# Eight columns of the conditioning product moved from VectorE to TensorE, x in four transfers, a shorter Newton step

## The chip, the cores and the metric

The kernel runs on one core of a Trainium2 chip. The time is the device time of one execution in microseconds, the median of several runs. In the views, PE is TensorE's matmuls, PEld its weight loads, DVE is VectorE, ACT ScalarE, POOL GpSimd, and SP the engine whose queue issues the transfers.

## What is computed

One layer of a streaming encoder on x of 512 tokens by 1024 features: a token-mixing half and a half with retrieved experts, each behind a normalization that is conditioned by a vector c. What the change touches is the conditioning and the norms:

```python
ada = c @ w_ada[layer] + b_ada[layer]
shift1, scale1, gate1, shift2, scale2, gate2 = [a[:, None, :] for a in jnp.split(ada, 6, axis=-1)]
h = rms_norm(x, g_norm1[layer]) * (1.0 + scale1) + shift1
z = h @ w_in[layer]
```

with `rms_norm(x, g) = x * rsqrt(mean(x * x) + EPS) * g`. ada has 6 x 1024 elements; the kernel holds it as 48 columns of 128.

## The kernel before

Features lie on the partitions, tokens along the free axis. x comes transposed as eight blocks `xs[:, d, :]` of 128 features by 512 tokens. `layer` is recorded as a program whose order on each engine a scheduler sets, within the dependencies; stretches that must keep their order are pinned.

The first stage (lines 241 to 285) makes the modulated input in two parts, `hh` and `hl`, a value rounded for the fast f32 format and what the rounding left, and multiplies it with five blocks of `w_in`, split in the same way into `whs` and `wls`. Each block and each feature block k gives three passes (`passes`, L171 to L173), 5 x 8 x 3 = 120 passes over 512 columns, into five banks `ps0` to `ps4`.

For feature block d the stage needs two columns of ada, the scale in column 8 + d and the shift in column d. `ada_col` (L102) loads 128 rows of the transposed w_ada as a tile `wada`, [128, 1024], and DVE multiplies it with c and sums along the row (L106). For that c is needed on all partitions: it comes as one row, `crow`, PE multiplies it with a column of ones (L253), and ACT copies the two halves into `cb` (L254). DVE then adds the bias (L266), makes a1 = (1 + scale) * g (L267) and, in `modulate`, x * a1 * r (L156); ACT adds the shift and rounds, giving `hh` (L157), and DVE makes `hl` (L158). The tiles `wada` rotate over four buffers, so a transfer waits for the product that read the buffer four columns before.

r, the reciprocal root, comes from `rsqrt` (L125): PE sums the squares over the partitions with a matrix of ones into `n1s` (L150, L151), ACT takes a logarithm, an exponential and a square, and DVE does one Newton step in three instructions (L132 to L134). It is used for the first norm (n1), for the norms of the index keys (nik), keys (nk) and queries (nq), and for the second norm (n2).

SP issues the transfers of this stage in order: `col` (constants by feature), `crow`, the eight blocks of x, then for each d two columns of w_ada and one block of w_in (`ws`), while there are any. The remaining 32 columns of ada come later, spread over the attention stages as background work.

After this stage come the queries, keys, scores and attention, the output projection, the second norm (from L500, where x is loaded again as `x2T`), and the experts, which take the larger part of the time.

## Time and profile before

| | us |
|---|---|
| median of 3 runs (1542.19 to 1545.64) | 1543.28 |
| the profiled execution | 1543.97 |
| its span, first to last instruction | 1542.2 |
| PE busy in it | 1496.3 (97%) |
| DVE busy | 1293.7 (84%) |
| ACT busy | 646.2 (42%) |

Busy time of PE is an upper bound, since matmuls are pipelined and their ends are modelled. The chain of waits that ended last runs over PE for 81% of the span, over DVE for 11%. All times of the rows below are microseconds from the start of the span, unless marked ns. A reader who looks at one stage should ask of each engine what it waited for there, and what its next instruction in order is.

### The profile page before, as it was taken

To read this page: it belongs to the slowest core of one execution; us is meant where nothing else is said; L and a number is where in the kernel's file an instruction comes from. 1 tells how busy PE (TensorE), PEld (TensorE's weight loads), DVE (VectorE), ACT (ScalarE), POOL (GpSimd) and SP (SyncE) were. 2 spreads that over 40 slices of the span, in tenths; PEclk is the share of its full clock that TensorE was granted. 3 is DMA by queue.
4 is the path that set the end of the run, shared out by engine and by line. 5 is a ranking of instruction groups with operands and counts; after the bars stand their busy time and mean duration, and the time that the engine had idled before them with its cause. 6 is when DMAs were issued, how large, how long until landed. Compare 5 with 4: busy or idle time off the path is not lost.

```text
span 1542.2 us, 22240 instructions
## 1 busy us (share of the span) xinstructions
PE 1496.3 (97%) x7889; PEld 1301.6 (84%) x7889; DVE 1293.7 (84%) x2672; ACT 646.2 (42%) x991; POOL 324.4 (21%) x318
## 2 busy tenths in 40 slices
PE   5999999999899999999999999999999999999998
PEld 3678788877799989899888999999999999998886
DVE  7799786667999999993778888888888888888887
ACT  4643555443345554463333333333333333333332
POOL 0000000000000000001123444444444444453320
PEclk8999999999999999999999999999999999999999
DMA  8422663532236656789889999999999999998884
GB/s 313 164 82 77 216 227 105 191 117 96 71 122 205 195 176 208 221 254 318 325 317 354 333 343 360 317 362 318 356 348 330 359 318 363 333 349 315 312 305 144
DMA packets 158545, 393.91 MB, mean 255 GB/s; under 512 B 13537, under 2 KB 68449, under 8 KB 158306
## 3 DMA queue, kind: packets, MB, share of 16 engines
q1 hardware_dynamic: 121570, 258.26, 48.3%
q0 software_dynamic: 36864, 134.23, 24.6%
q8 instruction: 62, 1.02, 0.3%
q14 instruction: 49, 0.40, 0.1%
HBM read 358.75 MB, written 33.69 MB: 254 GB/s over the span
## 4 chain that ended last, share of the span: by engine, by line
PE 81%; DVE 11%; DMA 5%; ACT 2%; issue 1%; SPq 0%; ACTq 0%; DVEq 0%
PE acc L806 28%; PE pse L555 6%; PE pse L554 6%; PE pse L553 6%; PE pse L569 4%; PE pse L571 4%; PE pse L570 3%; PE gm L666 3%; DMA v<-v 3%; DVE ule L533 2%; PE po L470 1%; DVE vl L798 1%; PE pso L171 1%; PE psgp L173 1%; PE psgp L171 1%
## 5 line engine op out<-in xcount | busy, mean ns | idle before, releaser
L731 POOL DMA_INDIRECT ur<-u,ei x128 | 156.3, 1221 | 603.5 <-DMA ad<-gelu 365.4
L806 PE MATMUL acc<-vl,Wh 128*128 128x512 f32 x768 | 237.1, 390 | 0.7 <-DVE vl L798 0.7
L806 PE MATMUL acc<-vh,Wl 128*128 128x512 f32 x768 | 237.3, 390 | 0.0
L806 PE MATMUL acc<-vh,Wh 128*128 128x512 f32 x768 | 236.8, 389 | 0.0
L739 POOL DMA_INDIRECT vr<-v,ei x128 | 165.2, 1290 | 213.7 <-DVE sacc L744 185.1
L798 DVE TENSOR_TENSOR vl<-v,vh 128x1024 fp32r<-128x1024 f32 x128 | 156.8, 1225 | 63.2 <-ACT vh L796 52.0
L555 PE MATMUL pse<-h2h,ule 128*128 128x384 f32 x552 | 185.2, 336 | 0.7 <-DVE ule L533 0.7
L553 PE MATMUL pse<-h2h,uhe 128*128 128x384 f32 x552 | 184.5, 334 | 0.6 <-ACT uhe L532 0.6
L554 PE MATMUL pse<-h2l,uhe 128*128 128x384 f32 x552 | 184.7, 335 | 0.0
L795 ACT ACTIVATE Wh<-gelu 128x384 fp32r<-128x384 f32 x106 | 55.6, 525 | 286.2 <-PE acc L806 161.9
L806 PEld LDWEIGHTS acc<-vl,Wh 128*128 128x128 f32 x768 | 143.9, 188 | 31.7 <-DVE vl L798 2.0
L806 PEld LDWEIGHTS acc<-vh,Wl 128*128 128x128 f32 x768 | 144.2, 188 | 29.9
L569 PE MATMUL pse<-h2h,uhe 128*128 128x384 f32 x472 | 167.8, 355 | 0.6 <-ACT gelu L578 0.6
L533 DVE TENSOR_TENSOR ule<-ue,uhe 128x1024 fp32r<-128x1024 f32 x128 | 155.8, 1217 | 13.7 <-ACT uhe L532 13.5
L571 PE MATMUL pse<-h2h,ule 128*128 128x384 f32 x472 | 161.1, 342 | 4.8 <-DVE ule L533 4.8
L744 DVE SCALAR_TENSOR_TENSOR sacc<-vr,wt,sacc 128x1024 f32<-128x1024 f32 x127 | 162.8, 1282 | 2.4
L806 PEld LDWEIGHTS acc<-vh,Wh 128*128 128x128 f32 x768 | 143.2, 188 | 24.7 <-ACT vh L796 0.3
L570 PE MATMUL pse<-h2l,uhe 128*128 128x384 f32 x472 | 159.1, 337 | 0.0
L532 ACT ACTIVATE uhe<-ue 128x1024 fp32r<-128x1024 f32 x128 | 134.5, 1051 | 57.8 <-PE pse L570 42.3
L733 DVE SCALAR_TENSOR_TENSOR ur<-ur,hx 128x1024 f32<-128x1024 f32 x128 | 150.6, 1218 | 0.4 <-DMA ur<-u,ei 0.4
L796 ACT ACTIVATE vh<-v 128x1024 fp32r<-128x1024 f32 x128 | 135.8, 1061 | 15.5 <-DMA v<-v 15.4
L553 PEld LDWEIGHTS pse<-h2h,uhe 128*128 128x128 f32 x552 | 103.6, 188 | 3.6 <-ACT uhe L532 1.0
(422 smaller groups left out, 2669.3 us busy)
## 6 DMA issues: line engine op xcount, KB each, us to landing
ue<-uT SPq DMA_DIRECT2D x128, 512.0 KB
v<-v SPq DMA_DIRECT2D x128, 512.0 KB
wada<-w_ada SPq DMA_DIRECT2D x48, 512.0 KB
gd<-st SPq DMA_DIRECT2D x24, 1024.0 KB
g<-gd SPq DMA_DIRECT2D x48, 512.0 KB
ad<-gelu SPq DMA_DIRECT2D x22, 192.0 KB
wgp<-w_in SPq DMA_DIRECT2D x8, 512.0 KB
wga<-w_in SPq DMA_DIRECT2D x8, 512.0 KB
```

The lines of the kernel that those rows point to most:

```text
L533: V.tensor_tensor(lo, src, hi.bitcast(F32), op=ALU.subtract)
L553: T.matmul(p, hi[:, k, :], h2h[:, k, :n], start=(k == 0), stop=False)
L554: T.matmul(p, hi[:, k, :], h2l[:, k, :n], start=False, stop=False)
L555: T.matmul(p, lo[:, k, :], h2h[:, k, :n], start=False, stop=(k == DT - 1))
L569: T.matmul(ps, hi[:, k, :], h2h[:, k, :ND], start=(k == 0), stop=False)
L570: T.matmul(ps, hi[:, k, :], h2l[:, k, :ND], start=False, stop=False)
L571: T.matmul(ps, lo[:, k, :], h2h[:, k, :ND], start=False, stop=(k == DT - 1))
L731: G.indirect_dma_start(out=ur, out_offset=None, in_=u, in_offset=bass.IndirectOffsetOnAxis(ap=ei3[:, k:k + 1], axis=0))
L739: G.indirect_dma_start(out=vr, out_offset=None, in_=v, in_offset=bass.IndirectOffsetOnAxis(ap=ei3[:, k:k + 1], axis=0))
L744: V.scalar_tensor_tensor(sacc, vr, wt[:, k:k + 1], sacc, op0=ALU.mult, op1=ALU.add)
L798: V.tensor_tensor(vl, vr, vh.bitcast(F32), op=ALU.subtract)
L806: T.matmul(acc[tb][i], x[:, t], y[:, i * 512:(i + 1) * 512], start=(c == 0 and n == 0), stop=(c == NEXP - 1 and n == 2))
```

## The change

Four edits:

- The columns of ada for the feature blocks 0 to 3 (`NPE = 4`) are made on PE. The host arranges their parts of w_ada so that a tile `wadp` holds, for each of the eight blocks k of c, 128 rows by 128 columns; PE takes each as the weights and one column of c, which now comes with `col`, as the moving operand (`ada_product`, L265 after the change), 8 matmuls into one column of the bank `pad`. DVE adds the bias from there. Blocks 4 to 7 stay with DVE as they were. The row `crow` and its two products follow only at d = 3, in one bank.
- x comes in four transfers of two blocks each, here and before the second norm, from an array arranged for it.
- The Newton step takes two instructions. Its factor -0.5 * scale is multiplied into the gains beforehand (L104, L105 of the changed kernel) and into the factor of rq.
- `col` is eight columns wider.

```diff
--- before.py
+++ after.py
@@ -59,7 +59,9 @@
 
 
 C_G1, C_G2, C_GQ, C_GK, C_GIK, C_SP, C_BADA = 0, 8, 16, 17, 18, 19, 23
-NCOLS = C_BADA + 48
+C_C = C_BADA + 48
+NCOLS = C_C + DT
+NPE = 4
 
 K_ID, K_IOTA, K_BLK, K_RC, NCONST = 0, 128, 256, 384, 448
 
@@ -67,7 +69,7 @@
 
 
 @with_exitstack
-def layer(ctx, tc, xT, cvec, w_ada, cols, consts, w_in, w_grp, w_up, w_out, w_pq, subk, u, uT, v, out):
+def layer(ctx, tc, xT, cvec, w_adap, w_ada, cols, consts, w_in, w_grp, w_up, w_out, w_pq, subk, u, uT, v, out):
     nc = tc.nc
     V, A, T, G = nc.vector, nc.scalar, nc.tensor, nc.gpsimd
     keep = ctx.enter_context(tc.tile_pool(name="keep", bufs=1, reuse_waits="tile"))
@@ -99,6 +101,9 @@
         ones = big.tile([P, P], F32, name="ones")
         V.memset(ones, 1.0)
 
+        V.tensor_scalar(col[:, C_G1:C_GQ], col[:, C_G1:C_GQ], -0.5 / D, None, op0=ALU.mult)
+        V.tensor_scalar(col[:, C_GK:C_GIK + 1], col[:, C_GK:C_GIK + 1], -0.5 / 64, None, op0=ALU.mult)
+
         def ada_col(j, pool, bufs):
 
             wt = pool.tile([P, D], F32, tag="wa", name=f"wada{j}", bufs=bufs)
@@ -130,8 +135,7 @@
             A.activation(r, t, AF.Exp, scale=-0.5)
             A.activation(t, r, AF.Square)
             V.scalar_tensor_tensor(t, ps, EPS / scale, t, op0=ALU.add, op1=ALU.mult)
-            V.tensor_scalar(t, t, -0.5 * scale, 1.5, op0=ALU.mult, op1=ALU.add)
-            V.tensor_tensor(r, r, t, op=ALU.mult)
+            V.scalar_tensor_tensor(r, t, -3.0 / scale, r, op0=ALU.add, op1=ALU.mult)
             return r
 
         def split(hi, lo, src):
@@ -241,29 +245,43 @@
                     tc.tile_pool(name="pst", bufs=1, space=PSUM, reuse_waits="tile") as pst:
                 xs = xp.tile([P, DT, S], F32, name="xs")
                 crow = wp.tile([P, D], F32, tag="wa", name="crow", bufs=3)[0:1, :]
-                nc.sync.dma_start(out=crow, in_=cvec)
                 ps = pst.tile([P, S], F32, name="n1s")
                 part = tmp.tile([P, S], F32, tag="nf", name="n1p")
                 for d in range(DT):
-                    nc.sync.dma_start(out=xs[:, d, :], in_=xT[d])
+                    if d % 2 == 0:
+                        nc.sync.dma_start(out=xs[:, d:d + 2, :], in_=xT[d // 2])
                     sq = square(part, xs[:, d, :], d, "n1sq")
                 square_sum(ps, part, sq)
-                for i in range(2):
-                    cp = pst.tile([P, S], F32, name=f"cp{i}")
-                    T.matmul(cp, ones[0:1, :], crow[:, i * S:(i + 1) * S], start=True, stop=True)
-                    A.copy(cb[:, i * S:(i + 1) * S], cp)
                 tc.keep_in_program_order(A.preload_act_table_set("natural_log_exp_and_others"))
                 both = lambda t, d: t.rearrange("p (i d) -> p i d", d=DT)[:, :, d]
                 rs, ws, accs = None, [], []
+                pad = pst.tile([P, 2 * DT], F32, name="pad")
+
+                def ada_product(i, j):
+
+                    wt = xp.tile([P, DT, P], F32, tag="wa", name=f"wadp{j}", bufs=4)
+                    nc.sync.dma_start(out=wt, in_=w_adap[i])
+                    for k in range(DT):
+                        T.matmul(pad[:, j:j + 1], wt[:, k, :], col[:, C_C + k:C_C + k + 1], start=(k == 0), stop=(k == DT - 1))
+
                 for d in range(DT):
-                    for j in (DT + d, d):
-                        ada_col(j, xp, 4)
+                    if d == NPE - 1:
+                        nc.sync.dma_start(out=crow, in_=cvec)
+                        for i in range(2):
+                            cp = pst.tile([P, S], F32, tag="cp", name=f"cp{i}")
+                            T.matmul(cp, ones[0:1, :], crow[:, i * S:(i + 1) * S], start=True, stop=True)
+                            A.copy(cb[:, i * S:(i + 1) * S], cp)
+                    for i, j in enumerate((DT + d, d)):
+                        if d < NPE:
+                            ada_product(2 * d + i, j)
+                        else:
+                            ada_col(j, xp, 4)
                     if d < len(begin):
                         ws.append(load(w_in[begin[d][0]], DT, f"s{d}", (wp, xp, xp, xq, xq)[d]))
                         accs.append(pst.tile([P, S], F32, name=f"ps{d}"))
                     if rs is None:
                         rs = rsqrt(ps, 1.0 / D, "n1")
-                    V.tensor_tensor(both(ada[:, 0:16], d), both(ada[:, 0:16], d), both(col[:, C_BADA:C_BADA + 16], d), op=ALU.add)
+                    V.tensor_tensor(both(ada[:, 0:16], d), both(pad if d < NPE else ada[:, 0:16], d), both(col[:, C_BADA:C_BADA + 16], d), op=ALU.add)
                     V.scalar_tensor_tensor(a1[:, d:d + 1], ada[:, DT + d:DT + d + 1], 1.0, col[:, C_G1 + d:C_G1 + d + 1],
                                            op0=ALU.add, op1=ALU.mult)
                     modulate(xs[:, d, :], rs, a1[:, d:d + 1], ada[:, d:d + 1], hh[:, d, :], hl[:, d, :], f"n1f{d}")
@@ -371,7 +389,7 @@
             for tb in range(TB):
                 T.transpose(qn[:, tb * NH:(tb + 1) * NH], qrow[:, tb * P:(tb + 1) * P], ident[0:NH, 0:NH])
             rq = rsqrt(qn, 1.0 / 64, "nq", "rq", TB * NH)
-            V.tensor_scalar(rq, rq, 0.125, None, op0=ALU.mult)
+            V.tensor_scalar(rq, rq, -0.5 / 64 * 0.125, None, op0=ALU.mult)
 
 
             pTh = lt.tile([P, 4, S], F32R, tag="bh", name="pTh")
@@ -500,8 +518,8 @@
         hx = k2.tile([P, D], F32, name="hx")
         xt = pre.enter_context(tc.tile_pool(name="xt", bufs=1, reuse_waits="tile"))
         xs = xt.tile([P, DT, S], F32, name="x2T")
-        for d in range(DT):
-            nc.sync.dma_start(out=xs[:, d, :], in_=xT[d])
+        for d in range(0, DT, 2):
+            nc.sync.dma_start(out=xs[:, d:d + 2, :], in_=xT[d // 2])
         tc.keep_in_program_order(A.preload_act_table_set("natural_log_exp_and_others"))
         nc.sync.dma_start(out=g2row.rearrange("o (j p) -> p (o j)", p=P), in_=ada[:, 40:48])
         sums = pac.tile([P, S], F32, tag="pac", name="n2s")
@@ -1004,10 +1022,12 @@
     zero = np.zeros((D, 60), w.dtype)
     w = np.concatenate([ik, k, iq, v, iw, zero, q, p, g], axis=1)
     cols = np.concatenate([_cols(g_norm1[0]), _cols(g_norm2[0]), _cols(np.tile(g_q[0], 2)), _cols(np.tile(g_k[0], 2)),
-                           _cols(np.tile(g_ik[0], 2)), s_pool[0].T, _cols(b_ada[0])], axis=1)
+                           _cols(np.tile(g_ik[0], 2)), s_pool[0].T, _cols(b_ada[0]), _cols(c)], axis=1)
+    wide = _blocks(w_ada[0][:, :2 * D])
     return {
-        "xT": np.ascontiguousarray(x[0].T).reshape(DT, P, S),
+        "xT": np.ascontiguousarray(x[0].T.reshape(DT // 2, 2, P, S).transpose(0, 2, 1, 3)),
         "cvec": c,
+        "w_adap": np.stack([wide[j] for d in range(NPE) for j in (DT + d, d)]),
         "w_ada": np.ascontiguousarray(w_ada[0].T),
         "cols": np.ascontiguousarray(cols),
         "consts": _consts(),
```

The order that results moves more than the lines do. First, PE's queue from its start to the first product with `hh`. In these rows `wadp8` is the tile of column 8, `pad` the bank of the columns, `n1s` the sum of squares, and a row with x7 stands for seven equal ones. Before:

```order
L253 MATMUL cp0_165<-crow_130,ones_85 128x512 [waits DMAHW1_49,DVE_49]
L253 MATMUL cp1_168<-crow_130,ones_85 128x512
L150 MATMUL n1s_132<-n1p_133,ones_85 128x512 [waits DVE_49]
L151 MATMUL n1s_132<-n1sq7_161,ones_85 128x512 [waits Activation_49]
L171 MATMUL ps0_184<-hh_87,whs0_179 128x512 [waits Activation_49]
L171 MATMUL ps1_214<-hh_87,whs1_209 128x512
L172 MATMUL ps0_184<-hl_88,whs0_179 128x512 [waits DVE_49]
```

Now, after the first matmul of column 8:

```order
L265 MATMUL pad_163<-col_59,wadp8_164 128x1 x7
L154 MATMUL n1s_133<-n1p_134,ones_85 128x512 [waits DVE_49]
L155 MATMUL n1s_133<-n1sq7_158,ones_85 128x512 [waits Activation_49]
L265 MATMUL pad_163<-col_59,wadp0_174 128x1 [waits DMAHW6_49]
L265 MATMUL pad_163<-col_59,wadp0_174 128x1 x7
L265 MATMUL pad_163<-col_59,wadp9_207 128x1 [waits DMAHW0_49,DVE_49]
L265 MATMUL pad_163<-col_59,wadp9_207 128x1 x7
L265 MATMUL pad_163<-col_59,wadp1_217 128x1 [waits DMAHW1_49]
L265 MATMUL pad_163<-col_59,wadp1_217 128x1 x7
L265 MATMUL pad_163<-col_59,wadp10_249 128x1 [waits DMAHW3_49,DVE_49]
L265 MATMUL pad_163<-col_59,wadp10_249 128x1 x5
L175 MATMUL ps0_190<-hh_89,whs0_185 128x512 [waits Activation_49]
```

The broadcast of c has left this place, column 8 stands ahead of the sum of squares, and columns 0, 9, 1 and most of 10 stand ahead of the first product with `hh`.

Second, DVE's queue around the fourth feature block (`n1f3`). `wls3` and `wls4` are the rounding rests of the weight blocks. Before:

```order
L156 SCALAR_TENSOR_TENSOR n1f2_245<-xs_129,a1_61,n1r_185 128x512 [waits DVE_49]
L139 TENSOR_TENSOR wls3_272<-ws3_270,whs3_271 128x1024 [waits DMAHW5_49,Activation_49]
L158 SCALAR_TENSOR_TENSOR hl_88<-n1f2_245,ada_60,hh_87 128x512 [waits Activation_49]
L266 TENSOR_TENSOR ada_60<-ada_60,col_59 128x2
L106 SCALAR_TENSOR_TENSOR wada12_304,ada_60<-wada12_304,cb_84 128x1024 [waits DMAHW6_49]
L267 SCALAR_TENSOR_TENSOR a1_61<-ada_60,col_59 128x1 [waits DVE_49]
L106 SCALAR_TENSOR_TENSOR wada4_307,ada_60<-wada4_307,cb_84 128x1024 [waits DMAHW7_49]
L156 SCALAR_TENSOR_TENSOR n1f3_279<-xs_129,a1_61,n1r_185 128x512 [waits DVE_49]
L139 TENSOR_TENSOR wls4_312<-ws4_310,whs4_311 128x1024 [waits DMAHW0_49,Activation_49]
L158 SCALAR_TENSOR_TENSOR hl_88<-n1f3_279,ada_60,hh_87 128x512 [waits Activation_49]
L266 TENSOR_TENSOR ada_60<-ada_60,col_59 128x2
```

Now:

```order
L160 SCALAR_TENSOR_TENSOR n1f3_333<-xs_131,a1_61,n1r_191 128x512 [waits DVE_49]
L143 TENSOR_TENSOR wls3_326<-ws3_324,whs3_325 128x1024 [waits DMAHW1_49,Activation_49]
L162 SCALAR_TENSOR_TENSOR hl_90<-n1f3_333,ada_60,hh_89 128x512 [waits Activation_49]
L111 SCALAR_TENSOR_TENSOR wada12_358,ada_60<-wada12_358,cb_84 128x1024 [waits DMAHW3_49,DMAHW2_49]
L111 SCALAR_TENSOR_TENSOR wada4_361,ada_60<-wada4_361,cb_84 128x1024 [waits DMAHW6_49,DMAHW4_49,DMAHW3_49]
L284 TENSOR_TENSOR ada_60<-ada_60,col_59 128x2 [waits DVE_49]
L285 SCALAR_TENSOR_TENSOR a1_61<-ada_60,col_59 128x1 [waits DVE_49]
L143 TENSOR_TENSOR wls4_366<-ws4_364,whs4_365 128x1024 [waits DMAHW4_49,Activation_49]
L160 SCALAR_TENSOR_TENSOR n1f4_373<-xs_131,a1_61,n1r_191 128x512 [waits DVE_49]
L111 SCALAR_TENSOR_TENSOR wada13_404,ada_60<-wada13_404,cb_84 128x1024 [waits DMAHW7_49,DMAHW5_49,DMAHW0_49]
L162 SCALAR_TENSOR_TENSOR hl_90<-n1f4_373,ada_60,hh_89 128x512 [waits Activation_49]
L111 SCALAR_TENSOR_TENSOR wada5_407,ada_60<-wada5_407,cb_84 128x1024 [waits DMAHW6_49,DMAHW0_49]
```

Before, the products of columns 12 and 4 stood ahead of `n1f3`, and before them those of columns 11 and 3. Now the add for block 3 waits for PE, and the products of columns 12 and 4 come behind `hl` of that block.

Third, SP's queue in the middle of the stage. Before:

```order
L105 DMA wada11_264<-w_ada 128x1024 [waits DMAHW3_49,DVE_49]
L105 DMA wada3_267<-w_ada 128x1024 [waits DMAHW4_49,DVE_49]
L165 DMA ws3_270<-w_in 128x1024 [waits DMAHW5_49,Activation_49]
L105 DMA wada12_304<-w_ada 128x1024 [waits DMAHW6_49,DVE_49]
L105 DMA wada4_307<-w_ada 128x1024 [waits DMAHW7_49,DVE_49]
L165 DMA ws4_310<-w_in 128x1024 [waits DMAHW0_49,Activation_49]
L105 DMA wada13_350<-w_ada 128x1024 [waits DMAHW1_49,DVE_49]
L105 DMA wada5_353<-w_ada 128x1024 [waits DMAHW2_49,DVE_49]
L105 DMA wada14_377<-w_ada 128x1024 [waits DMAHW3_49,DVE_49]
L105 DMA wada6_380<-w_ada 128x1024 [waits DMAHW4_49,DVE_49]
```

Now:

```order
L269 DMA crow_132<-cvec 1x1024
L263 DMA wadp11_304<-w_adap 128x1024 [waits DMAHW7_49,DMAHW0_49,PE_49]
L263 DMA wadp3_314<-w_adap 128x1024 [waits DMAHW1_49,PE_49]
L169 DMA ws3_324<-w_in 128x1024 [waits DVE_49]
L110 DMA wada12_358<-w_ada 128x1024 [waits DMAHW3_49,DMAHW2_49,PE_49]
L110 DMA wada4_361<-w_ada 128x1024 [waits DMAHW4_49,PE_49]
L169 DMA ws4_364<-w_in 128x1024 [waits DVE_49]
L110 DMA wada13_404<-w_ada 128x1024 [waits DMAHW7_49,DMAHW5_49,PE_49]
L110 DMA wada5_407<-w_ada 128x1024 [waits DMAHW6_49,DMAHW0_49,PE_49]
L110 DMA wada14_431<-w_ada 128x1024 [waits DVE_49]
```

The transfers of columns 12, 4, 13 and 5 waited for DVE's products of the columns whose buffers they take; they now wait for PE's products of columns 10, 2, 11 and 3.

## Rows read from the trace of the kernel before

**Rows 1.** Busy time of each engine in stretches of the span: the stretch and its length; busy time and, in brackets, the number of instructions of PE, PEld, DVE, ACT and POOL; the granted TensorE clock as a share of full speed; the mean share of the DMA engines; GB/s.

```profile
3.00:11.50 8.50, 3.55 (x4) 0.93 (x4) 4.15 (x6) 6.08 (x10) 0.00 (x0) 1.00 0.94 337
11.50:23.40 11.90, 3.65 (x5) 1.20 (x5) 10.60 (x19) 5.63 (x9) 0.00 (x0) 0.78 1.03 413
23.40:40.00 16.60, 15.06 (x52) 10.79 (x53) 16.60 (x31) 5.16 (x6) 0.00 (x0) 0.85 0.79 273
40.00:55.30 15.30, 15.30 (x66) 11.90 (x65) 12.58 (x26) 5.74 (x8) 0.00 (x0) 1.00 0.85 307
...
80.00:140.00 60.00, 60.00 (x253) 45.98 (x252) 59.64 (x157) 24.32 (x38) 0.00 (x0) 1.00 0.25 83
...
200.00:1542.00 1342.00, 1318.09 (x7156) 1167.99 (x7155) 1119.62 (x2271) 547.41 (x824) 323.13 (x304) 1.00 0.77 268
```

**Rows 2.** ACT's instructions in order of time: start, duration, line, output and input; in brackets the idle time before it and what ended it. `hh` is shown for the feature blocks 0, 2, 3 and 7.

```profile
14.50 1.06 ACT L138 ACTIVATE whs<-ws 128x1024 fp32r<-128x1024 f32 x1 [2.12 <-DMA ws<-w_in]
15.47 0.67 ACT L129 ACTIVATE n1t<-n1s,eps 128x512 f32<-128x512 f32 x1
...
16.83 0.63 ACT L131 ACTIVATE n1t<-n1r 128x512 f32<-128x512 f32 x1
...
22.60 0.72 ACT L157 ACTIVATE hh<-n1f,ada 128x512 fp32r<-128x512 f32 x1 [3.21 <-DVE n1f L156]
...
31.17 0.72 ACT L157 ACTIVATE hh<-n1f,ada 128x512 fp32r<-128x512 f32 x1 [4.12 <-DVE n1f L156]
...
36.06 0.72 ACT L157 ACTIVATE hh<-n1f,ada 128x512 fp32r<-128x512 f32 x1 [3.10 <-DVE n1f L156]
...
51.21 0.72 ACT L157 ACTIVATE hh<-n1f,ada 128x512 fp32r<-128x512 f32 x1 [2.00 <-DVE n1f L156]
```

**Rows 3.** PE in the first stage: first its instructions in order of time, as in rows 2 (the last row is the load of the next stage's first weights); then two groups of its matmuls by line and shape, with busy time in us and mean duration in ns.

```profile
11.50 2.07 PE L150 MATMUL n1s<-n1p,ones 128*128 128x512 f32 x2 [4.95 <-DVE n1p L146]
13.37 1.75 PE L151 MATMUL n1s<-n1sq,ones 128*128 128x512 f32 x2
23.37 1.22 PE L171 MATMUL ps<-hh,whs 128*128 128x512 f32 x2 [8.25 <-ACT hh L157]
...
36.84 1.20 PE L171 MATMUL ps<-hh,whs 128*128 128x512 f32 x4 [0.42 <-ACT hh L157]
...
56.13 0.19 PEld L171 LDWEIGHTS psq<-hh,whq 128*128 128x128 f32 x1
...
L150 PE MATMUL n1s<-n1p,ones 128*128 128x512 f32 x2 | 2.1, 1140 | 5.0 <-DVE n1p L146 5.0
...
L151 PE MATMUL n1s<-n1sq,ones 128*128 128x512 f32 x2 | 1.8, 981 | 0.0
```

**Rows 4.** DVE from 11.5 to 56 us in groups by line and shape (busy us, mean ns, idle time before them), and one instruction of its timeline, `hl` of feature block 3.

```profile
L106 DVE SCALAR_TENSOR_TENSOR wada<-wada,cb 128x1024 f32<-128x1024 f32 x16 | 19.4, 1212 | 0.5 <-DMA wada<-w_ada 0.5
L139 DVE TENSOR_TENSOR wls<-ws,whs 128x1024 fp32r<-128x1024 f32 x5 | 6.1, 1215 | 0.7 <-ACT whs L138 0.7
L156 DVE SCALAR_TENSOR_TENSOR n1f<-xs,a,n1r 128x512 f32<-128x512 f32 x8 | 5.9, 739 | 0.0
L158 DVE SCALAR_TENSOR_TENSOR hl<-n1f,ada,hh 128x512 fp32r<-128x512 f32 x8 | 5.9, 739 | 0.8 <-ACT hh L157 0.8
...
37.09 0.73 DVE L158 SCALAR_TENSOR_TENSOR hl<-n1f,ada,hh 128x512 fp32r<-128x512 f32 x1
```

**Rows 5.** Passes and loads of PE by price, from its timeline and groups: eight loads of `po` (L470) in one row, and their group; four transpose passes (L372); a load at half clock; two passes over 512 columns at full clock.

```profile
261.74 0.97 PEld L470 LDWEIGHTS po<-vw,pT 128*128 128x128 f32 x8 [0.72 <-ACT pT L468]
...
L470 PEld LDWEIGHTS po<-vw,pT 128*128 128x128 f32 x160 | 21.0, 191 | 5.9 <-ACT pT L468 4.7
...
93.66 0.32 PEld L372 LDWEIGHTS nq<-con,nqr 8*128 8x128 f32 x4 [0.36 <-ACT nqr L369]
...
24.66 0.33 PEld L173 LDWEIGHTS ps<-hh,wls 128*128 128x128 f32 x1
...
38.82 0.40 PE L173 MATMUL ps<-hh,wls 128*128 128x512 f32 x1
39.05 0.39 PE L172 MATMUL ps<-hl,whs 128*128 128x512 f32 x1
```

**Rows 6.** Stretches of 2 us of the first stage, columns as in rows 1.

```profile
2.00:4.00 2.00, 1.20 (x2) 0.70 (x3) 0.00 (x0) 0.03 (x1) 0.16 (x1) 1.00 0.73 177
4.00:6.00 2.00, 2.00 (x3) 0.45 (x2) 0.04 (x1) 1.26 (x2) 0.00 (x0) 1.00 0.95 308
6.00:8.00 2.00, 0.55 (x1) 0.00 (x0) 1.34 (x2) 1.43 (x3) 0.00 (x0) 1.00 0.95 354
8.00:10.00 2.00, 0.00 (x0) 0.00 (x0) 1.42 (x3) 1.91 (x5) 0.00 (x0) 1.00 0.94 307
10.00:12.00 2.00, 0.50 (x1) 0.50 (x2) 1.42 (x3) 1.97 (x3) 0.00 (x0) 1.00 1.00 411
12.00:14.00 2.00, 2.00 (x3) 0.67 (x2) 1.94 (x3) 0.39 (x1) 0.00 (x0) 1.00 1.03 422
...
18.00:20.00 2.00, 0.00 (x0) 0.00 (x0) 2.00 (x5) 1.06 (x1) 0.00 (x0) 0.56 1.03 412
...
28.00:30.00 2.00, 2.00 (x9) 1.59 (x9) 2.00 (x6) 0.00 (x0) 0.00 (x0) 0.88 0.99 385
```

**Rows 7.** From the timeline around the second norm: the transfers of `x2T` and DVE's first use of it, the second instruction of the Newton step, and PE's wait behind the norm.

```profile
294.80 3.95 SPq L504 DMA_DIRECT2D x2T<-xT  x8
...
300.58 0.74 DVE L511 SCALAR_TENSOR_TENSOR x2T<-pso,ada,x2T 128x512 f32<-128x512 f32 x1
...
341.16 0.43 DVE L133 TENSOR_SCALAR n2t<-n2t 128x512 f32<-128x512 f32 x1
...
343.91 0.73 PE L553 MATMUL pspq<-h2h,uhpq 128*128 128x512 f32 x2 [2.71 <-ACT h2h L157]
```

## The prediction

> **What bounds the kernel now.** I read the windows by stage first. From 200 us on PE is busy 1318 of 1342 us, and from 80 to 140 us all of it [rows 1], so a microsecond by which the first stage ends sooner or later reaches the end. The change lies in that first stage, the conditioned projection of the first five weight blocks. Its windows show three limits in turn: DMA moves over 400 GB/s at full share until 23.4 us, DVE is busy all 16.6 us of the next stretch, and PE all 15.3 us of the last [rows 1]. The times of ACT's `hh` show the pace: 22.60 us for the first feature block, 31.17 for the third, 36.06 for the fourth, 51.21 for the last [rows 2]. PE's first product with `hh` starts at 23.37; from 36.84 it never waits, and the next stage's weights are loaded at 56.13 [rows 3]. So up to 36.8 us the stage hangs on the chain that makes `hh`, mostly on DVE, whose largest group is sixteen column products of 1.21 us [rows 4]; afterwards on PE.
>
> **What a column costs on PE.** This decides. A column is 8 matmuls, each in two passes, each pass with its own load of 128 x 128 f32 weights for one moving column. No row shows one moving column. The nearest is `po` (L470), the same f32 weights with 64: eight loads stand in 0.97 us, each 0.19 long, so one follows another after (0.97 - 0.19) / 7 = 0.111 us [rows 5]. The pass is set by its load, not by its columns, so I take 0.111: 16 x 0.111 = 1.78 us a column. Below lies the transpose pass of L372, four in 0.32 us with 0.14 each: 0.06, or 0.98 us a column; above, the same pass at half clock, 0.222 or 3.55 us (a load shows 0.33 there, 0.19 at full clock [rows 5]). [...]
>
> **The chain to the first `hh`.** (a) x in four transfers: in its rows of 2 KB the three windows from 4 to 10 us show 308, 354 and 307 GB/s, the next ones, in rows of 4 KB, 411 and 422 [rows 6]. x and `col` are 2.14 MB, so 5.2 us instead of 6.5. Landing follows the last byte by 1.1 us: the 3.71 MB up to the first weight block have moved at 13.3 us by these windows, and ACT had it at 14.50 [rows 2]. With first bytes at 2.8 us, the last of x lands at 9.1, the first ada column at 10.4, the first weight block at 12.9 (1.6 sooner). (b) But PE now runs the first column ahead of the sum of squares. It starts at 10.4 and at half clock ends at 13.95; the sum, whose operand is ready at 11.0, waits 2.9 us for it. Before, the sum ran from 11.50 to 15.12, its first two passes 1.14 us long on the mean and its last two 0.98 [rows 3], so I let the clock rise at 14.8; the sum then ends at 16.35. (c) ACT's three steps (15.47 to 17.46 before [rows 2]) end at 18.5. DVE's Newton step is an instruction shorter, 0.34 on this chain, but its second instruction stands behind the adds of the second block, which need columns 9 and 1: PE gives them at 21.4. So the first `hh` comes at 23.2 instead of 22.6, and PE's first product with it at 24.0 instead of 23.4. The DMA lead is gone.
>
> **From there to the fourth block.** PE runs the products in order. The third `hh` waits for column 2, which stands behind ten passes of the blocks before: 31.1 us, as before (31.17). Then come PE's 13 passes for that block at 0.233 (38.82 to 39.05 is the interval of two [rows 5]), 3.0 us, the second broadcast of c, 0.85 (two passes of 0.43, moved here from a time when PE idled), and columns 11 and 3, 3.55, before DVE may add, scale and modulate and ACT round: 40.6 us instead of 36.06. That is **+4.6 us**, of which the two columns are 3.55.
>
> **From the fourth block to the last.** DVE's order has the products of blocks 4 to 7 behind the fourth `hl`. Its end moves from 37.83 [rows 4] to 42.4. Then DVE has eight column products (9.1 to 9.7 us), two weight splits, four modulations and three `hl`, in all 17.1 us to the last `hh`, at 59.5. Before, it had six products and one split left there, 13.4 us to 51.21. **+3.8 us**: the products that PE took left DVE idle earlier, at waits for `pad`, and those that stayed did not move up. SP holds them back too: the buffers of columns 12 and 4 come free with PE's columns 10 and 2, those of 13 and 5 with 11 and 3 (37.7 and 39.5 us), but they land before DVE reaches them. The tail from the last `hh` to the end of the stage is 5.9 instead of 5.0, PE having a little of block 6 left: **+0.9**.
>
> Sum of the stage: 4.6 + 3.8 + 0.9, about **+9.2 us** (the queues carried forward in the same way over the order before end at 56.2 us; over the new one at 65.4). PE's side agrees: 24.0, plus 120 passes x 0.233 = 28.0, plus the 3.25 columns still to come, 5.8, plus two broadcasts 1.7, plus waits of 0.8, 0.8, 1.6 and 2.8 is 65.5.
>
> **Elsewhere.** In the second norm PE waits 2.71 us for a chain through the removed multiply-add; its 0.43 us and the gap behind make 0.46 [rows 7], which I take as **-0.46 us**. The two norms of keys and index keys and the small one of queries lie where PE has matmuls to run: nothing, at most 0.9 gained. x's second load starts at 294.80 us, nearly 6 us ahead of its first use at 300.58 [rows 7]: nothing, and if that cover were gone 1.3 us gained. The two scalings of `col` fall into DVE's first idle time: nothing.
>
> The profiled execution took 1543.97 us, 0.7 above the median of 1543.28. 1543.97 + 9.2 - 0.46 = **1552.7 us**. A difference of 0.2%, 3.1 us, is about what a measurement of this kernel can tell from none.
>
> **Rivals.**
> [...]
> - **Loads are cheaper**, as in L372, 0.061 a pass: the stage ends at 59.8, +3.6, 1547.1. Against: that row is a transpose.
> [...]
> - **Faster: DVE is the stage's limit and is simply relieved.** Eight products of 1.21 us gone, 9.7 us, the columns falling into the 8.25 us in which PE idled before 23.37 [rows 3]; PE then starts at 20 and needs its 28 us, the stage ends at 48, 8 us sooner: 1535.5. For it: DVE has no free time from 23.4 to 40 us [rows 1]. It decides if a column costs PE under some 0.3 us and DVE's later products move up; the new order forbids the second and the load rows the first.
>
> **Numbers.** The case of the sum 0.50, the clock 0.28, cheaper loads 0.10, no change 0.07, faster 0.05. The first three are slower by more than 0.2%: 0.88. The range runs from cheap loads, less 1 us, to the clock's upper end: 1546 to 1560. It leaves out the last two cases and a clock that stays half still longer.
>
> **What would show it.** Right: sixteen passes of a `pad` column 1.7 to 1.8 us apart at full clock; the sum of squares starting at about 14 us; the fourth `hh` near 40 us; DVE idle before the adds of blocks 2 and 3 and packed after 42; the stage's end near 65 us and all later stages shifted by that. Wrong: a column in under 1 us, a first `hh` before 21 us, or the fourth before 36. [...]

## The result and the profile after

The changed kernel takes 1565.06 us (median of 4 runs, 1564.69 to 1568.47) where the kernel before takes 1544.46: a ratio of 1.0145, 95% interval 1.0128 to 1.0161. It is slower, by 20.6 us; forecast were +9 and at most +16. The ratios here and below are estimated from all runs, and differ from the quotient of the two medians by up to 0.0018. The profiled execution took 1564.84 us with a span of 1563.1, 20.9 longer than before.

The first stage alone shows the loss. The next stage's first weights are loaded at 77.94 us, 56.13 before [rows 3]: +21.8. The row of the changed kernel:

```profile
77.94 0.19 PEld L175 LDWEIGHTS psq<-hh,whq 128*128 128x128 f32 x1
```

At the end of the attention the lag is 19.7 (last load of `po` 284.3, before 264.6), in the second norm PE waits 2.24 us instead of 2.71 [rows 7], and at the end it is 20.9.

ACT's `hh` of the changed kernel, columns as in [rows 2]; the first row holds blocks 0 and 1:

```profile
29.33 1.38 ACT L161 ACTIVATE hh<-n1f,ada 128x512 fp32r<-128x512 f32 x2 [9.07 <-DVE n1f L160]
39.50 0.72 ACT L161 ACTIVATE hh<-n1f,ada 128x512 fp32r<-128x512 f32 x1 [7.84 <-DVE n1f L160]
53.22 0.72 ACT L161 ACTIVATE hh<-n1f,ada 128x512 fp32r<-128x512 f32 x1 [5.24 <-DVE n1f L160]
...
72.11 0.72 ACT L161 ACTIVATE hh<-n1f,ada 128x512 fp32r<-128x512 f32 x1 [1.81 <-DVE n1f L160]
```

Forecast were 23.2 for the first, 31.1, 40.6 and 59.5. So the first is 6.1 us late, the third 8.4, the fourth 12.6, and there it stays: from the fourth to the last pass 18.9 us, as forecast. All that was missed lies ahead of the fourth `hh`. What DVE waits for there, in us in all, times and the longest:

```profile
DVE ada L284 <- PE pad L265: 31.8, 4, 10.8
```

PE's column products and their surroundings, in order of time (a column is a row of 16 passes; x32 are two):

```profile
10.10 3.55 PE L265 MATMUL pad<-col,wadp 128*128 128x1 f32 x16 [10.10 <-DMA wadp<-w_adap]
13.50 2.05 PE L154 MATMUL n1s<-n1p,ones 128*128 128x512 f32 x2
15.35 1.92 PE L155 MATMUL n1s<-n1sq,ones 128*128 128x512 f32 x2
17.06 3.41 PE L265 MATMUL pad<-col,wadp 128*128 128x1 f32 x16
20.72 6.99 PE L265 MATMUL pad<-col,wadp 128*128 128x1 f32 x32 [0.25 <-DVE ada L284]
...
36.45 1.84 PE L265 MATMUL pad<-col,wadp 128*128 128x1 f32 x16
...
47.29 4.71 PE L265 MATMUL pad<-col,wadp 128*128 128x1 f32 x32
```

The same 16 passes take 3.41 us at 17.06 and 1.84 at 36.45: 0.213 and 0.115 a pass, a factor of nearly two. Those are TensorE's pass times at two levels of its clock, half and full: in e4 (below) the same passes took 0.213 us each where the granted clock is 0.50 (56 to 58 us) and 0.113 where it is 1.00 (52 to 54 us). By the pass times it was at half clock without a break from the first column to about 36 us. Windows of the changed kernel, columns as in [rows 1]:

```profile
17.10:30.50 13.40, 12.89 (x61) 12.72 (x60) 4.73 (x10) 4.07 (x6) 0.00 (x0) 1.00 0.46 164
...
36.20:39.50 3.30, 3.30 (x22) 2.46 (x20) 1.11 (x4) 0.00 (x0) 0.00 (x0) 1.00 0.08 14
39.50:46.50 7.00, 6.84 (x15) 4.51 (x15) 1.77 (x2) 2.20 (x3) 0.00 (x0) 0.51 0.37 143
46.50:49.90 3.40, 3.40 (x25) 2.64 (x25) 0.00 (x0) 0.59 (x1) 0.00 (x0) 0.99 0.00 0
49.90:59.90 10.00, 9.07 (x27) 7.10 (x27) 7.71 (x14) 2.06 (x3) 0.00 (x0) 0.50 0.53 181
59.90:77.90 18.00, 18.00 (x78) 14.27 (x77) 14.11 (x27) 6.10 (x9) 0.00 (x0) 1.00 0.81 292
```

Two things are to be read here. PE is busy in 12.89 of 13.40 us of the first window and slow all the same: a busy PE is no sign of a fast one. And the clock column says 1.00 there, in a stretch whose passes take twice their time; until the first change that it records (0.89 in 38 to 40 us), the pass duration is the better witness. From 36 us the two agree: the clock is up for 3.3 us (1.00), down for 7 (0.51), up for 3.4 (0.99), in which the columns 11 and 3 start, down for 10 (0.50), and up from 59.9 on (1.00), when only passes over 512 columns are left.

### The profile page after: what moved, and what is told of

Same layout as the page of the kernel before. It is cut to its first block, busy times and chain, and to the rows that moved or that the text cites. A ratio compares the mean times of both kernels' runs of the same rounds, so it can differ in the third digit from the quotient of the medians.

```text
span 1563.1 us, 22464 instructions
## 1 busy us (share of the span) xinstructions
PE 1526.5 (98%) x8017; PEld 1330.3 (85%) x8017; DVE 1284.6 (82%) x2653; ACT 645.9 (41%) x991; POOL 326.8 (21%) x318
## 4 chain that ended last, share of the span: by engine, by line
PE 81%; DVE 12%; DMA 3%; ACT 2%; issue 1%; SPq 0%; ACTq 0%; DVEq 0%
PE acc L824 31%; PE pse L573 6%; PE pse L571 6%; PE pse L572 6%; PE pse L587 4%; PE pse L589 4%; PE pse L588 4%; PE gm L684 3%; DVE bias L365 2%; PE pad L265 2%; DVE ule L551 1%; DMA v<-v 1%; DVE m L364 1%; PE po L488 1%; PE pso L175 1%
## 5 line engine op out<-in xcount | busy, mean ns | idle before, releaser
L551 DVE TENSOR_TENSOR ule<-ue,uhe 128x1024 fp32r<-128x1024 f32 x128 | 155.9, 1218 | 13.6 <-ACT uhe L550 13.4
L815 DVE TENSOR_TENSOR Wl<-gelu,Wh 128x384 fp32r<-128x384 f32 x106 | 59.3, 559 | 60.4 <-ACT Wh L813 60.2
```

What stands on the lines that cost most here:

```text
L551: V.tensor_tensor(lo, src, hi.bitcast(F32), op=ALU.subtract)
```

## Experiments

Times are medians; each ratio is to the kernel before on the same chip. "Stage end" is the load of the next stage's first weights, 56.1 before and 77.9 in the changed kernel. Theory A is the clock: one-column passes neither lift it nor hold it. Theory B is the queues: the order costs the time at any clock.

**Taking the columns back.** e1 is the kernel before with the two small edits, so it differs from the changed kernel by the columns alone (c is broadcast at the start again).

```diff
-                        if d < NPE:
-                            ada_product(2 * d + i, j)
-                        else:
-                            ada_col(j, xp, 4)
+                        ada_col(j, xp, 4)
```

> The changed kernel with the columns taken back to VectorE (c broadcast at the start as before); x in four transfers and the two-instruction Newton step stay. [...] Theory C (the small edits): a part of the loss comes from the four transfers or the scaled gains; then this kernel stays above 1547.

Measured: 1540.31 us, ratio 0.9975 (0.9964 to 0.9986), stage end 54.5. This is faster than both kernels, and 1.7 us below 1542 to 1545 us, the range that theories A and B both give without the columns; the columns on PE cost 20.6 + 3.4 = 24 us. Theory C falls, and the small edits gain more than the forecast's 0.46. Each alone (e5: L132 to L134 and the gains; e6: the two loops of transfers, as the change has them):

> The kernel before with the two-instruction Newton step and the scaled gains alone. The forecast's price was -0.46 us in the second norm and nothing elsewhere: 1543.2 beside a before of 1543.7. Theory S: the step also stands on the chain to the first hh (0.34 us) and on the norms of keys and queries: up to -1.5 us. It cannot be told from no change if it is under 1.5.

> The kernel before with x in four transfers, here and before the second norm, alone. The columns back on VectorE with both small edits gave -3.4 us, 1.4 of them by the end of the first stage. Theory S: the transfers' lead of 1.3 to 1.6 us moves the whole DVE-bound first stage: -1.4 to -2.5 us, 1541 to 1542.5, stage end near 54.8. The forecast's rival reading, that the lead is lost on the way: 1543 to 1544, stage end 56.

Measured: e5 1541.03 us, 0.9986 (0.9975 to 0.9997), stage end 56.1; e6 1541.56 us, 0.9986 (0.9976 to 0.9997), stage end 54.9. So x in four transfers moves the stage by 1.2 us. The Newton step moves the first `hh` (20.94 us, before 22.60) but not the stage's end, in which PE is the limit (busy 15.30 of 15.30 us [rows 1]); its gain is 0.5 to 3.9 us by the interval, and what exceeds the second norm's half microsecond can't be placed.

**More moving columns behind the same loads.** In e2 each column of c moves 64 times beside itself (`S // (2 * NPE)`; `slots` is the bank `pad` in eight parts), and no other work is added:

```diff
-                        T.matmul(pad[:, j:j + 1], wt[:, k, :], col[:, C_C + k:C_C + k + 1], start=(k == 0), stop=(k == DT - 1))
+                        T.matmul(slots[:, j // DT, j % DT, :], wt[:, k, :], col[:, C_C + k:C_C + k + 1].to_broadcast([P, S // (2 * NPE)]), start=(k == 0), stop=(k == DT - 1))
```

> The changed kernel with c repeated 64 times as the moving operand of each column product, so every pass streams 64 columns instead of one behind the same load; the sum of squares is pinned behind column 8, as the changed kernel has it. Everything else, loads, order and transfers, is the same. Theory A: what TensorE streams decides its clock, the loads do not count; it now rises by 16 us and stays, a pass keeps its 0.111 us, the stage ends at 64 to 68 us instead of 78.2, and the kernel takes 1550 to 1555 us (the forecast's own sum was 1552.7). Theory B: the queues' order costs the time; nothing changes in them, 1562 to 1567. A second rival, that only long passes over 512 columns lift the clock: also 1562 to 1567, with passes 0.22 us apart until the first products with hh.

Measured: 1557.04 us, 1.0087 (1.0072 to 1.0102), stage end 65.4 in the profiled run of 1554.4. PE streams 64 times as many columns and the kernel is 8 us faster than the changed one:

```profile
16.51 1.54 PE L155 MATMUL n1s<-n1sq,ones 128*128 128x512 f32 x2
17.89 1.90 PE L265 MATMUL pad<-col,wadp 128*128 128x64 f32 x16
20.03 3.79 PE L265 MATMUL pad<-col,wadp 128*128 128x64 f32 x32 [0.25 <-DVE ada L286]
...
25.51 0.73 PE L175 MATMUL ps<-hh,whs 128*128 128x512 f32 x2 [1.00 <-ACT hh L161]
26.08 2.80 PE L265 MATMUL pad<-col,wadp 128*128 128x64 f32 x20
...
28.00:30.00 2.00, 2.00 (x8) 1.78 (x8) 1.16 (x2) 0.00 (x0) 0.00 (x0) 0.50 0.81 260
```

The clock rose within the last passes of the sum (1.54 us for two, 1.92 in the changed kernel) and stayed up under three columns (0.118 us a pass); it fell once, from 28 to 31 us (granted 0.50 in 28 to 30), behind an idle microsecond before 25.51 and more wide passes. The time is 2 us above theory A's range, the stage within it; theory B and the second rival (1562 to 1567) fall. Two things are mixed in here besides: the order on DVE changed a little too, and whether the clock rose because of the wide passes is open. e12 below has the changed kernel's order, nearly, and an idle product with which the clock rose behind a narrow column as well (e11).

**Fewer columns, and other ones.** e3 has `NPE = 2`. e4 gives PE the columns of blocks 4 to 7, among passes over 512 columns (`ON_PE = range(DT - NPE, DT)` in place of `d < NPE`).

> The changed kernel with columns on TensorE for feature blocks 0 and 1 only (NPE = 2): four columns instead of eight. [...] Theory B at full clock: half of the forecast's 9.2, stage end 59 to 62, 1546 to 1549.

> As the changed kernel, but the four blocks whose columns TensorE makes are 4 to 7 instead of 0 to 3; c is broadcast at d = 0, and VectorE makes the columns of blocks 0 to 3. The column passes now stand among passes over 512 columns. [...] Theory B (the first chain's queues are the loss): the first four blocks come as before, 1544 to 1550.

Measured: e3 1555.79 us, 1.0086 (1.0069 to 1.0104), stage end 65.2; e4 1569.75 us, 1.0178 (1.0162 to 1.0195), stage end 80.6. Theory A had e3's columns at half clock, the first `hh` near 30 us, the stage's end at 62 to 67 and 1549 to 1554 us. The stage is where it had it, the time 2 us above, and it came there by another path: the clock was up for the second column (1.85 us), and the first `hh` came at 25.62 us. That the number fits is luck. e4 goes 2 us beyond theory A's worse form, in which the clock falls even there (1562 to 1568 us), and speaks against B: its first `hh` comes at 22.76, as before, and it is the slowest kernel here. Both show one-column passes losing a clock that was up. First e3, PE's columns and two windows, then two rows of columns of e4:

```profile
17.22 1.85 PE L265 MATMUL pad<-col,wadp 128*128 128x1 f32 x16
...
20.04 3.07 PE L265 MATMUL pad<-col,wadp 128*128 128x1 f32 x16
...
20.00:22.00 2.00, 2.00 (x13) 1.96 (x12) 1.93 (x5) 0.59 (x1) 0.00 (x0) 0.66 0.94 299
22.00:24.00 2.00, 2.00 (x7) 1.52 (x7) 0.59 (x1) 0.00 (x0) 0.00 (x0) 0.50 0.55 225
```

```profile
50.86 3.63 PE L266 MATMUL pad<-col,wadp 128*128 128x1 f32 x32
54.74 6.82 PE L266 MATMUL pad<-col,wadp 128*128 128x1 f32 x32 [0.25 <-DVE ada L285]
```

Two columns in 3.63 us, the next two in 6.82, with 0.25 us between them: 0.113 and 0.213 us a pass. In e3 the clock was up behind the sum of squares, at 17.2, from the same place and with the same passes as in the changed kernel, where it was not (1.85 and 3.41 us for the column).

**Is the missed rise the rule?** The changed kernel again (e9), and with one idle f32 product of 512 columns ahead of the sum of squares (e11) or behind each of the first six columns (e10):

```diff
+                        if i == 0 and k == DT - 1:        # e11; e10: behind each column with i < 6
+                            tc.keep_in_program_order(T.matmul(fill, ones, xs[:, 0, :], start=True, stop=True))
```

> The changed kernel once more, unaltered: whether the sum of squares fails to lift the clock every time. With two blocks on TensorE the same four passes at the same place (13.66 to 17.2 us) did lift it, and the columns behind ran 0.111 us a pass until 21. If the changed kernel's long half level (to 36 us) is the rule, 1564 to 1569 us and the same trace; if it is chance, a run with a rise at 17 us, a stage end near 75 us and about 1561 us.

> The changed kernel with one such idle product, right behind column 8 and ahead of the sum of squares, so that six f32 passes over 512 columns stand there. Theory A: the clock rises before the columns 0, 9, 1 and falls within 3 to 4 us, since one-column passes do not hold it (seen with two blocks on TensorE, and behind the last two columns in the changed kernel); one or two columns are 1.7 us shorter, the filler costs 1.7: stage end 75 to 79 us, 1561 to 1566 us. Rival (one-column passes hold the level that they find): columns at 1.78 us until the first hh, stage end 66 to 69, 1552 to 1556 us.

> The changed kernel with one idle f32 product over 512 columns (ones times x, into the bank that the broadcast of c uses later) behind each of the first six columns. The columns, their order and their one moving column stay. [...] Rival (the clock is not what costs the time, or it can't be held so): six fillers of 0.86 to 1.7 us more on the path, stage end 84 to 88 us, 1571 to 1576 us.

Measured: e9 1565.25 us, three runs at 1564.8 to 1566.4 and one at 1557.44; its profiled run (1566.41) has the same half level, to 36.7 us. By their times seven of the changed kernel's eight runs have it; of the exception there is no profile. e11 1565.27 us, 1.0126 (1.0103 to 1.0150), stage end 74.5, theory A's case (half a microsecond below its range): the clock rose, and was lost again under one-column passes, as the 2.13 and 5.54 us for one and two columns and the windows show:

```profile
20.20 2.13 PE L266 MATMUL pad<-col,wadp 128*128 128x1 f32 x16
22.59 5.54 PE L266 MATMUL pad<-col,wadp 128*128 128x1 f32 x32 [0.26 <-DVE ada L287]
...
22.00:24.00 2.00, 1.75 (x17) 1.66 (x16) 0.92 (x3) 1.41 (x2) 0.00 (x0) 1.00 0.32 70
24.00:26.00 2.00, 2.00 (x12) 2.00 (x12) 0.00 (x0) 0.00 (x0) 0.00 (x0) 0.55 1.01 395
```

The rival (one-column passes hold what they find) falls. The stage ends 3.4 us sooner than in the changed kernel and the time is the same: what follows the stage takes from 1483 to 1489 us in the profiles here, 1489.4 in e11, where the clock fell once more (granted 0.83 from 80 to 90 us). So the stage end says more of the columns than the time does. e10 took 1568.89 us, 1.0153 (1.0133 to 1.0174), stage end 81.5, 3.6 us later than the changed kernel. It is a miss for both theories: A, by which the idle products lift the clock by 18 us and hold it through the columns, had 1556 to 1560 us, the rival 1571 to 1576. The clock rose at about 19 us, as e11's did, and fell in the window from 22 to 24 (granted 0.73) although a product over 512 columns stood behind each column:

```profile
19.54 1.84 PE L266 MATMUL pad<-col,wadp 128*128 128x1 f32 x16
21.24 1.10 PE L268 MATMUL fill<-xs,ones 128*128 128x512 f32 x2
22.18 2.75 PE L266 MATMUL pad<-col,wadp 128*128 128x1 f32 x16
24.79 2.05 PE L268 MATMUL fill<-xs,ones 128*128 128x512 f32 x2
```

That one such product in a column's time would hold it was my addition to theory A, and it is wrong.

**The clock up all the way.** e12 has e2's wide columns, e11's idle product ahead of the sum, and VectorE's product of column 12 pinned behind the fourth block's `n1f`, near the changed kernel's order. e13 is e12 without that pin.

```diff
-                            ada_col(j, xp, 4)
+                            m = ada_col(j, xp, 4)
+                            if j == DT + NPE:
+                                tc.keep_in_program_order(m)
```

> Columns 64 wide as before, one idle f32 product over 512 columns between column 8 and the sum of squares, so that the clock is up before the columns, and VectorE's product of column 12 pinned behind n1f of the fourth block as in the changed kernel's order. Theory A: with the clock up from about 19 us to the end of the stage this is the forecast's own case: from the sum of squares on, columns at 1.8 us; fourth hh near 41 us plus the filler (1.9 us), 19 us from there to the last hh, 5 to 6 us from it to the end: stage end 64 to 68 us, 1552 to 1557 us. If the clock falls again on the way, 2 to 4 us more. Rival (the excess over the forecast was not the clock): stage end over 74, 1562 or more.

> The same without the pin: VectorE makes columns 12 and 4 while it waits for the fourth block's columns. The forecast's step +3.8 says that products standing behind the fourth hl cost what is left of VectorE's work: with two of them moved up, fourth to last hh takes some 15 to 16 us instead of 19, the stage ends 2 to 3 us sooner, 1550 to 1555 us. If VectorE's late products are not the limit there, no difference.

Measured: e12 1553.31 us, 1.0057 (1.0035 to 1.0078), stage end 65.1; e13 1549.33 us, 1.0044 (1.0026 to 1.0062), stage end 62.5. e12's windows, with PE's columns and ACT's fourth and last `hh`:

```profile
18.80:32.30 13.50, 12.99 (x96) 11.69 (x94) 7.54 (x15) 5.29 (x7) 0.00 (x0) 1.00 0.67 245
...
41.50:65.10 23.60, 22.41 (x94) 16.70 (x94) 20.43 (x39) 8.21 (x11) 0.00 (x0) 1.00 0.83 294
...
19.20 1.89 PE L266 MATMUL pad<-col,wadp 128*128 128x64 f32 x16
21.34 3.79 PE L266 MATMUL pad<-col,wadp 128*128 128x64 f32 x32 [0.25 <-DVE ada L290]
...
37.75 3.79 PE L266 MATMUL pad<-col,wadp 128*128 128x64 f32 x32
...
42.75 0.73 ACT L161 ACTIVATE hh<-n1f,ada 128x512 fp32r<-128x512 f32 x1 [4.31 <-DVE n1f L160]
...
60.17 0.72 ACT L161 ACTIVATE hh<-n1f,ada 128x512 fp32r<-128x512 f32 x1 [2.00 <-DVE n1f L160]
...
65.10 0.19 PEld L175 LDWEIGHTS psq<-hh,whq 128*128 128x128 f32 x1
```

Every column behind the sum now takes 1.9 us, and 13.5 us hold 96 of PE's instructions where the changed kernel's 13.4 hold 61. The stage ends 12.8 us sooner than in the changed kernel (77.9 - 65.1), with the idle product's 1.8 us in it, and where the forecast's sum had it (65.4). The rival of e12 falls: the excess over that sum is the clock, to within some 2 us. The plainest pair is e11 and e12, which have the same idle product in the same place, with the clock up behind the sum, and differ in the width of the columns and the pin: under one moving column it fell at 24.2 us (granted 0.55 in 24 to 26 us), under 64 it stayed (1.00). In e13 the products of columns 12 and 4 stand ahead of the fourth `n1f`; from the fourth `hh` (42.41) to the last (57.90) pass 15.5 us, against 17.4 in e12. The first column began 1.2 us sooner in e13's profile (9.97 against 11.19), so of the 2.6 us between the stage ends 1.4 are left for the moved products, half of what was expected, from one profile of each.

**Two attempts at a better kernel.** e7 gives PE only block 1's columns, wide, in its idle time behind the sum of squares; e8 traces VectorE's columns of block 4 + d beside those of block d, with c broadcast at the start.

```diff
+ON_PE = [1]                                                    # e7
+   for i, j in enumerate((DT + d, d, DT + d + NPE, d + NPE)) if d < NPE else ():   # e8
```

> The kernel with columns on VectorE, x in four transfers and the short Newton step, but the two columns of feature block 1 alone made on TensorE, 64 columns of c wide, in the time in which TensorE idles behind the sum of squares. [...] Theory B (waits of VectorE's queue for TensorE's columns cost what the products cost): 1540 to 1543.

> As the kernel with wide columns (stage end 65.6), but c is broadcast at the start and the columns that stay on VectorE are traced beside those of TensorE (block 4 + d with block d), so VectorE's eight products stand in the time in which it waited for columns. The forecast's step +3.8 (they stand behind the fourth hl and do not move up) and its second broadcast then vanish: the fifth to eighth hh come 3 to 4 us after one another's predecessors' passes at most, TensorE is the limit; stage end 59 to 62, 1547 to 1552 us. Theory D (VectorE's later products were not the limit): stage end still 64 to 66, 1554 to 1558.

Measured: e7 1546.05 us, 1.0019 (1.0008 to 1.0030), stage end 57.5; e8 1566.52 us, 1.0155 (1.0140 to 1.0171), stage end 78.9. Both miss (e7's range was 1537.5 to 1539.5 us by theory A and 1540 to 1543 by B). In e7 the columns are hidden (16.48 to 20.46), but the first `hh` is not sooner (21.80, in e1 21.02) and the fourth later (37.21, in e1 34.42): DVE's queue there has the two products of block 4 ahead of the fourth `n1f` (36.44), so what was taken off DVE came back as order. In e8 the clock was not up behind the sum of squares, and the wide columns there stayed at half clock:

```profile
16.52 7.09 PE L266 MATMUL pad<-col,wadp 128*128 128x64 f32 x32
23.87 7.09 PE L266 MATMUL pad<-col,wadp 128*128 128x64 f32 x32 [0.25 <-DVE ada L285]
```

0.222 us a pass for 14 us, where e12 has 0.118. So passes with 64 columns stayed at the high level where they found it (e12, e13) and did not leave the low one here. e8 can't say what interleaving is worth.

## Why the prediction was wrong

- **The direction and the place were right**: slower, all of it in the first stage, on the chain that goes through `pad`.
- **The price of a column was right at full clock**: 0.111 us a pass was taken from `po` [rows 5]; 16 passes took 1.84 us in the changed kernel at 36.45, and two columns 3.63 in e4, 0.113 a pass. At half clock a pass took 0.213 to 0.222 us. Cheaper loads, 0.061 us a pass, are out. And no run shows columns that are all but free, the case of no change (0.07): the least of these rows is 0.113 us a pass.
- **The step that failed** is in part (b), "so I let the clock rise at 14.8". The level was taken from the kernel before, where the last two passes of the sum were shorter than the first two (1.75 us against 2.07 [rows 3]). There the clock rose in the last of them; the forecast kept that time, though it had moved the start of the sum from 11.50 to 13.95 and put a column ahead of it. In the changed kernel the four passes ran at half clock to their end (2.05 and 1.92 us for two, 13.50 to 17.27), and what follows is not idle time as before, but 13 us of one-column passes under which the clock did not rise (0.213 to 0.218 us each). The columns 0, 9 and 1 took 10.4 us instead of 5.3 and the first `hh` came 6.1 us late; the first passes with `hh`, the thirteen ahead of the fourth block, and part of the second broadcast and of the columns 11 and 3, at half clock too, made that 12.6 by the fourth. **+4.6 us was forecast there; it was +17.2** (53.22 - 36.06). e12 and e2 show that it is the clock. Why it did not rise in the sum is open (below).
- **The clock's case had the right cause and too small a size.** It had a chance of 0.28 and about 1558 us: the half level from 18 to 30 us, as in the kernel before (granted 0.56 in 18 to 20, 0.88 in 28 to 30 [rows 6]), or from the start to 28, and a stage end of 69.4 or 72.0. It was kept small because PE would not be idle under the columns. That argument is refuted: PE is busy 12.89 of 13.40 us at half clock. And no run of the changed kernel with a profile shows a half level that ends at 28 or 30 us and does not come back, on which the upper end of the range, 1560, stands; it was down to 36, and down again from 39.5 to 46.5 (0.51) and 49.9 to 59.9 (0.50), the last time in the middle of one-column passes.
- **+3.8 and +0.9 us held.** From the fourth `hh` to the last 18.9 us instead of 15.15, +3.7; from the last to the stage's end 5.8 instead of 4.9, +0.9. That the products behind the fourth `hl` set the first of them is supported by DVE's queue, which is busy in 16.89 of the 17.00 us from 54.3 on, and by e13, which moved two of them up and ended 1.4 us sooner.
- **The sum was right for the case it was made for**: 65.4 us of stage and 1552.7 of time; with the clock up e12 gave 65.1 and 1553.31. That it agrees so closely is in part luck: e12 carries an idle product of 1.8 us, its first column began 1.1 us later, and it has one weight split less behind the fourth `hh`. The agreement is good to some 2 us.
- **The small edits**: -0.46 us in the second norm came as forecast (2.71 to 2.24). The transfers of x were booked inside the chain and the rest at nothing; on the kernel before, both edits together gave -3.4 us (-1.6 in the stage). Against a stage that the clock had lengthened by 12.8 this was not the mistake, but "nothing" was too little.
- **A reading that carries nothing**: DMA moves over 400 GB/s until 23.4 us only from 11.5 us on; before, the row has 337 [rows 1].

What stays open: why the clock is up at the end of the four f32 passes of the sum in the kernel before, e2, e3, e4 and e7, and not in the changed kernel's two profiles and in e8. e3 has the same head as the changed kernel. e4 and e8 have the same passes up to there, broadcast, sum, broadcast: the last broadcast took 1.12 us in e4 and 2.07 in e8. So that the column ahead of the sum kept the clock from rising is not shown. What the low level cost is shown, by e12.

## What to carry to other kernels

Moving the matrix-vector product to TensorE put passes there that were nearly all weight load (PEld busy in 12.72 of 13.40 us); price such passes at both levels of its clock (0.113 and 0.213 us here), and do not assume the high level from the time at which an earlier, denser stretch had it. If such passes must stand on a critical chain, let them stream more columns than they need behind the same loads, with dense work ahead of them, with which the clock stayed up in e12 and e13 (0.118 us a pass), fell once in e2 and was not up in e8 (0.222), and look at the duration of one pass, not at the busy share, to see the level. And where a queue's order is set by a scheduler, work taken off an engine is only a gain if what stays behind moves up. No kernel here with columns on TensorE was as fast as the one before (e13 1.0044, e7 1.0019); the fastest is e1, without them.

## What the runs showed of the hardware

- One-column f32 passes with a 128 x 128 load each, back to back (12.89 of 13.40 us busy): 0.213 to 0.218 us each at half clock and no rise in 13 us; at full clock 0.113 to 0.115, and a fall to half clock in the middle of them in the changed kernel, e3, e4 and e11 (granted 1.00 in 52 to 54 us of e4, 0.50 in 56 to 58).
- The same passes with 64 moving columns cost nearly the same (0.118 at full clock, 0.222 at half clock), stayed at full clock from the end of the sum to the end of the stage in e12 and e13 (granted 1.00), lost it once in e2 (28 to 31 us, granted 0.50 in 28 to 30), and did not bring it back in 14 us of e8.
- The clock column read 1.00 in stretches at the start of the span in which passes took nearly twice their time (17.1 to 30.5 us of the changed kernel, 0.213 to 0.218 us against 0.115 at 36.45).
